# Two six-block groups of each down projection as seven products of halves, between plain groups of 4, 3 and 3 blocks

## The chip, the cores and the metric

The kernel runs on one core of a Trainium2 chip. The metric is the device time of one launch in microseconds. Its engines are named as the profile names them: PE is TensorE (matmuls; PEld is its weight load), DVE is VectorE, ACT is ScalarE, POOL is GpSimd, SP is SyncE, which here issues the DMAs.

## The reference, cut to what matters

One decoder layer over 1024 tokens of width 1024, all in float32. Two of its stages are gated feed-forward blocks with 2816 = 22 x 128 hidden columns; the change lies in them. Between them stands the mixer (attention and a linear recurrence, merged), behind the second the last stage (a gated embedding and the last norm).

```python
def swiglu(x, w_in, w_out):
    gate, up = jnp.split(x @ w_in, 2, axis=-1)
    return (jax.nn.silu(gate) * up) @ w_out
...
        h = h + 0.5 * swiglu(rms_norm(h, norm_ffn1[layer]), w_ffn1_in[layer], w_ffn1_out[layer])
...
        h = h + 0.5 * swiglu(rms_norm(h, norm_ffn2[layer]), w_ffn2_in[layer], w_ffn2_out[layer])
...
```

## The kernel before, in words

Activations are kept transposed: a block is a tile of 128 features (partitions) by 1024 tokens, in two halves of 512 tokens (`HALVES`). Each operand is split into a high and a low part of a narrower type: a product of one 128x128 weight block with 512 tokens is three matmuls (high with high, high with low, low with high). ACT casts the high part (`whi`, `xh`, `gh`), DVE subtracts it to get the low part (`wlo`, `xl`, `gl`).

A half step is one call of `swiglu(n, ...)`, n = 1 for FFN1 and 2 for FFN2. It has two stages.

*Gates.* The 22 hidden blocks are worked off one after the other, as gate units. Units 0 and 1 are plain (`product8`). Units 2 to 21 go by `product7`, a Strassen-like scheme: gate and up columns are the two halves on the one side, the two token halves on the other, and seven products of half the depth (four blocks, three passes, so 12 matmuls each, 84 in a unit) replace eight. Its operands are sums: `wsum` of weights (DVE, then split into parts) and `xsum` of inputs (made once, in class `Halves`). Products are numbered 1 to 7; `a`, `b`, `e`, `g`, `f` are PSUM banks, product 4 adds into product 1's bank after ACT has copied that out as `p`; `u` tiles are partial results that DVE adds. A table `before` hangs extra work on a step of the unit. What to do with the four results is told by an object: `Gated` multiplies by the norm (`rstd`), applies silu and the gate product on POOL (`u*rstd`, `a*u`), and spills the block to DRAM (`aspill`). In FFN1 the norm is not known yet when units 0 and 1 are done, so `keep` copies their sums out of PSUM on ACT, and `rest` evaluates them later, in unit 3 at steps 4 and 6. In FFN2 `all` evaluates units 0 and 1 at once.

*Down.* The 22 blocks are summed in groups (`GROUPS`, 6, 6, 5 and 5 blocks before). For each group and each of the eight output columns c, `gemm` runs blocks x 3 passes x 2 halves matmuls into two PSUM banks, and DVE then adds half of them to the residual tile `hT[c]` (one SCALAR_TENSOR_TENSOR a half). Blocks come back from DRAM as `araw` (`fetch`) and are split into `gh`, `gl` (`part`), one block a column while the previous group runs. In the final group each eviction is followed by the next stage's input (`xgh` on ACT, `xgl` on DVE) and the squares for its norm (`sq` on ACT, added to `acc` on POOL, the very last half on DVE). The next stage's first weights are split in the last two columns: on DVE for the mixer, on POOL for the last stage (`ple`).

`stats_later(acc, a, b)` puts two steps on a side list that PE's k loop counts off: transposes of `acc` with ident, a reduction and a reciprocal square root on DVE (`st_v`, `st_r`), transposes of `st_r`, and the broadcast `rstd`. Before, FFN2's end calls it twice.

DVE and ACT instructions run in the order in which the code is written (class `InOrder`; their line in the profile is therefore always L44). The instructions of PE, POOL and SP are ordered by a scheduler. Pools bound what runs ahead: 38 block tiles of 128x1024, three raw weight tiles (`wraw`), seven split weight tiles, five scratch tiles, eight PSUM banks. `ensure` prepares weights one or two steps ahead in the order of a plan.

In the profile PE's plain matmuls carry line L260 (`gemm_steps`), those of `product7` L280, those of the last stage L1212.

## Time and profile before

| | |
|---|---|
| median of three runs (2228.82 to 2231.6) | 2228.9 us |
| profiled execution, its own time | 2230.69 us |
| its span | 2228.9 us |
| PE busy | 2192.9 us (98%) |
| DVE busy | 1352.5 us (61%) |
| ACT busy | 716.2 us (32%) |
| POOL busy | 442.9 us (20%) |
| FFN1's down stage in the trace | 455.5 to 694.8 us |
| FFN2's down stage in the trace | 1846.05 to about 2085.3 us |

The chain of waits follows the work that ended last back to the beginning; a row of PE there says that nothing but PE itself held it up in that time. The timeline gives each instruction's start and length, and in brackets how long the engine had idled before and for whom. The granted clock is a share of TensorE's full speed of 2.4 GHz.

### The profile page before, as it was taken

The page shows a single profiled execution, that of the slowest core. Times are in us where ns is not written, and L with a number is a line of the kernel's source. Part 1 is how long each engine was busy: PE and PEld are TensorE (multiplying, and loading weights), DVE is VectorE, ACT ScalarE, POOL GpSimd, SP SyncE. Part 2 cuts the span into 40 slices and gives each one's busy share as a digit, 9 for nine tenths or more (in the row PEclk, how much of TensorE's full clock was granted, in tenths as well). Part 3 has the DMA queues.
Part 4 walks back from the last instruction along what each step waited for, and adds up shares of the span by engine and source line. Part 5 has one row for each costly group of instructions (what it writes and reads, how often), then busy time and mean ns, then how long its engine had stood idle before and what let it go on. Part 6 is the DMA issues. An engine that isn't in the chain of part 4 may idle for free.

```text
span 2228.9 us, 26842 instructions
## 1 busy us (share of the span) xinstructions
PE 2192.9 (98%) x10644; PEld 1821.4 (82%) x10644; DVE 1352.5 (61%) x1947; ACT 716.2 (32%) x1191; POOL 442.9 (20%) x233
## 2 busy tenths in 40 slices
PE   8899999999999999999999999999999999999997
PEld 7687888888888888888888888878888888888887
DVE  6777777753345665466674354677777775334545
ACT  6423222231123443322222233332222223122444
POOL 0222222200012000122220122212222220001443
PEclk9999999999999999999999999999999999999999
DMA  9223222272223121111124434212222227221322
GB/s 279 85 86 112 89 85 78 89 266 93 76 79 123 39 67 57 35 32 36 32 67 133 148 108 142 84 58 86 85 85 85 85 96 256 95 70 51 95 75 87
DMA packets 258448, 213.37 MB, mean 96 GB/s; under 512 B 16049, under 2 KB 231442, under 8 KB 258322
## 3 DMA queue, kind: packets, MB, share of 16 engines
q1 hardware_dynamic: 258322, 211.65, 29.7%
q8 instruction: 84, 1.38, 0.3%
q14 instruction: 42, 0.34, 0.1%
HBM read 163.37 MB, written 49.82 MB: 96 GB/s over the span
## 4 chain that ended last, share of the span: by engine, by line
PE 85%; DVE 9%; ACT 2%; issue 1%; POOL 1%; DMA 1%; SPq 0%; ACTq 0%; DVEq 0%; POOLq 0%
PE ps L260 43%; PE ps L280 32%; PE ps L1212 3%; DVE at L44 2%; DVE wlo L44 1%; PE ps L392 1%; PE ps L897 1%; DVE rk L44 1%; PE ps L845 1%; DVE hT L44 1%; DVE xsum L44 1%; PE ps L1251 1%; DVE wsum L44 1%; ACT whi L44 1%; PE ps L884 1%
## 5 line engine op out<-in xcount | busy, mean ns | idle before, releaser
L280 PE MATMUL ps<-xh,whi 128*128 128x512 f32 x800 | 312.8, 391 | 4.0 <-ACT p L44 4.0
L280 PE MATMUL ps<-xh,wlo 128*128 128x512 f32 x800 | 311.8, 390 | 0.6 <-DVE wlo L44 0.5
L280 PE MATMUL ps<-xl,whi 128*128 128x512 f32 x800 | 312.0, 390 | 0.0
L44 ACT CAST whi<-wraw 128x1024 fp32r<-128x1024 f32 (+3 forms) x190 | 174.7, 924 | 346.8 <-PE ps L260 293.5
L658 POOL TENSOR_TENSOR u<-u,rstd 128x1024 f32<-128x1024 f32 x44 | 121.3, 2757 | 653.2 <-ACT a L44 428.6
L44 DVE SCALAR_TENSOR_TENSOR hT<-ps,hT 128x512 f32<-128x512 f32 x128 | 82.5, 686 | 243.0 <-PE ps L260 243.0
L260 PE MATMUL ps<-gh,wlo 128*128 128x512 f32 x704 | 217.1, 389 | 0.0
L260 PE MATMUL ps<-gl,whi 128*128 128x512 f32 x704 | 217.0, 389 | 0.0
L260 PE MATMUL ps<-gh,whi 128*128 128x512 f32 x704 | 216.8, 389 | 0.0
L44 DVE TENSOR_TENSOR wlo<-wraw,whi 128x1024 fp32r<-128x1024 f32 (+3 forms) x174 | 188.6, 1088 | 46.4 <-ACT whi L44 43.4
L260 PE MATMUL ps<-xgh,whi 128*128 128x512 f32 x608 | 197.1, 403 | 0.0
L44 DVE TENSOR_TENSOR wlo<-wsum,whi 128x1024 fp32r<-128x1024 f32 x80 | 134.2, 1678 | 94.5 <-ACT whi L44 94.5
L260 PE MATMUL ps<-xgh,wlo 128*128 128x512 f32 x608 | 190.6, 392 | 0.0
L260 PE MATMUL ps<-xgl,whi 128*128 128x512 f32 x608 | 190.2, 392 | 0.0
L280 PEld LDWEIGHTS ps<-xh,whi 128*128 128x128 f32 x800 | 150.5, 188 | 37.7 <-ACT p L44 6.1
L280 PEld LDWEIGHTS ps<-xh,wlo 128*128 128x128 f32 x800 | 150.6, 188 | 32.8 <-DVE wlo L44 1.5
L280 PEld LDWEIGHTS ps<-xl,whi 128*128 128x128 f32 x800 | 150.6, 188 | 30.9
L44 ACT CAST whi<-wsum 128x1024 fp32r<-128x1024 f32 x80 | 84.2, 1052 | 271.1 <-DVE wsum L44 271.1
L260 PEld LDWEIGHTS ps<-gh,wlo 128*128 128x128 f32 x704 | 132.0, 188 | 27.7 <-DVE wlo L44 0.4
L260 PEld LDWEIGHTS ps<-gl,whi 128*128 128x128 f32 x704 | 132.1, 188 | 27.5
L260 PEld LDWEIGHTS ps<-gh,whi 128*128 128x128 f32 x704 | 132.0, 188 | 27.6
L260 PEld LDWEIGHTS ps<-xgl,whi 128*128 128x128 f32 x608 | 113.6, 188 | 23.9
(253 smaller groups left out, 3832.5 us busy)
## 6 DMA issues: line engine op xcount, KB each, us to landing
wraw<-in_w_ffn_in_dram SPq DMA_DIRECT2D x88, 512.0 KB, 3.9
aspill<-a SPq DMA_DIRECT2D x44, 512.0 KB, 2.9
araw<-aspill SPq DMA_DIRECT2D x44, 512.0 KB, 4.9
wraw<-in_w_in_dram SPq DMA_DIRECT2D x34, 512.0 KB, 3.9
hspill<-hT SPq DMA_DIRECT2D x24, 512.0 KB, 6.3
wraw<-in_w_ffn_out_dram SPq DMA_DIRECT2D x32, 384.0 KB, 4.2
hT<-hspill SPq DMA_DIRECT2D x24, 512.0 KB, 10.2
wraw<-in_w_ffn_out_dram SPq DMA_DIRECT2D x32, 320.0 KB, 3.2
```

The lines of the kernel that those rows point to most:

```text
L44: return self.tc.keep_in_program_order(method(*args, **kwargs))
L260: nc.tensor.matmul(ps[b], wk, xk[:, HALVES[b]], start=(k == 0 and n == 0), stop=(k == kc - 1 and n == 2))
L280: nc.tensor.matmul(ps, a[:, ks], b, start=first and k + n == 0, stop=k == 3 and n == 2, skip_group_check=not first)
L392: nc.tensor.matmul(ps[b], w, xs[b][part], start=i == 0 and m == 0, stop=i == DC - 1 and m == 2)
L658: nc.gpsimd.tensor_mul(self.u, self.u, R["rstd"])
L845: nc.tensor.matmul(ps[:, off:(m + 1) * 256], q[j][0][:, n * P:(n + 1) * P], ak[j][part][:, k0:k1], start=part == 0, stop=part == 1)
L884: nc.tensor.transpose(pt[:, a * P:(a + 1) * P], s[:, (4 * j + a) * P:(4 * j + a + 1) * P], ident)
L897: nc.tensor.matmul(po[64 * j:64 * j + 64, m * P:(m + 1) * P], av[:, (n - 1 + kb) * P + 64 * j:(n - 1 + kb) * P + 64 * j + 64], st[:, (2 * ...
L1212: nc.tensor.matmul(ps, wk, xk[:, sl], start=(k == 0 and n == 0), stop=(k == kc - 1 and n == 2))
L1251: nc.tensor.matmul(self.pp, wps[k][j][:, c * P:(c + 1) * P], pt[k][m][:, self.sl], start=(k + i == 0), stop=(k + i == 3))
```

## The change

The groups become (4, plain), (6, halves), (3, plain), (6, halves), (3, plain). A halves group runs `product7` on pairs of output columns c and c + 4, with the six blocks as two threes: seven products of three blocks and three passes, 63 matmuls, for two columns. Its weights are prepared by `halves_step`, now for any size (768 columns of raw weights, sums of 384). A new class `Down` adds the four results to `hT` with seven SCALAR_TENSOR_TENSOR a unit.

The inputs of a halves group are three pairs of blocks. While the plain group ahead of it runs, `pairs_steps` loads them (`get`), splits their quarters (`put`), forms their four sums of 512 columns each (`sums`), and splits these (`rest`). The sums are made on DVE for the first halves group and on POOL for the second. While a halves group runs, the three blocks of the next plain group are fetched and split, at steps of its second to fourth unit.

The last gate unit fetches and splits blocks earlier, and `hT` tiles are loaded three ahead in place of all at once. In FFN1 the copies of unit 1's sums (`us[1].keep`) move behind product 3 of unit 2, and `us[1].rest` moves from unit 3, step 6, to unit 4, step 4. In FFN2 `us[1].all` moves to the same step of unit 2. At FFN2's end the statistics are made once.

```diff
-    GROUPS = (6, 6, 5, 5)
+    GROUPS = ((4, False), (6, True), (3, False), (6, True), (3, False))
...
+        for gn, halves in GROUPS:
+            for c in PAIRED if halves else range(DC):
+                yield f"{'half' if halves else 'down'}{n}.{f0}.{c}", gn, load_cols(w_down, c * P, P, f0, gn)
...
+            eng = eng or nc.vector
...
-            6: [lambda: squares((4, 5)), lambda: load_rows((6, 7))], 7: [lambda: ensure(where["gate1.2"], 2)]}))
+            6: [lambda: squares((4, 5)), lambda: load_rows((6, 7))], 7: [lambda: ensure(where["gate1.2"], 2)]})
         return {
-            2: {1: [xt[3].p13], 3: [lambda: squares((6, 7)), first_r], 5: [first_rstd]},
-            3: {4: [us[0].rest], 6: [us[1].rest]}}
+            2: {1: [xt[3].p13], 3: [lambda: squares((6, 7)), first_r, lambda: us[1].keep(*ps)], 5: [first_rstd]},
+            3: {4: [us[0].rest]}, 4: {4: [us[1].rest]}}
...
+        def pairs_steps(f0, gn, pairs):
+            half = gn // 2
+
+            def get(j):
+                for k in range(2):
+                    f = f0 + half * k + j
+                    fetch(f)
+                    pairs[j].x[k] = araw.pop(f)
+
+            def put(j):
+                pairs[j].put_seven()
+                pairs[j].sums(nc.gpsimd if f0 > GROUPS[0][0] else nc.vector)
+
+            def rest(j):
+                pairs[j].p24()
+                pairs[j].p13()
+
+            order = ((get, 0), (get, 1), (put, 0), (put, 1, get, 2), (rest, 0), (put, 2), (rest, 1), (rest, 2))
+            return [[lambda f=f, j=j: f(j) for f, j in zip(o[::2], o[1::2])] for o in order]
...
+            def add(self, k, b, *terms):
+                h = hT[self.c + 4 * k][:, HALVES[b]]
+                for t in terms:
+                    nc.vector.scalar_tensor_tensor(h, t, 0.5, h, ALU.mult, ALU.add)
+
+            def c11(self, a):
+                self.add(0, 0, a)
+
+            def c22(self, g, u4):
+                self.add(1, 1, g, u4)
+
+            def c12(self, f, u4):
+                self.add(0, 1, f, u4)
+
+            def c21(self, g, u2):
+                self.add(1, 0, g, u2)
...
+            if halves:
+                todo = [f1 + i for i in range(GROUPS[gi + 1][0])]
+                for c in range(4):
+                    before = {}
+                    if c == 1:
+                        before = {5: [lambda: fetch(todo[0])]}
+                    elif c == 2:
+                        before = {2: [lambda: part(todo[0]), lambda: fetch(todo[1])], 6: [lambda: part(todo[1]), lambda: fetch(todo[2])]}
+                    elif c == 3:
+                        before = {3: [lambda: part(todo[2])]}
+                    product7(f"half{n}.{f0}.{c}", pairs[f0], Down(c), before)
+                del pairs[f0]
+                continue
...
+                pairs[f1] = [Halves() for _ in range(GROUPS[gi + 1][0] // 2)]
+                steps = pairs_steps(f1, GROUPS[gi + 1][0], pairs[f1])
...
-        us[1].all(*ps)
-        return {}
+        return {2: {3: [lambda: us[1].all(*ps)]}}
 
     hT, xg, acc = swiglu(2, xt, R_PLE, lambda c, h: None, second_units)
-    stats_later(acc, 9, 6)
-    stats_later(acc, 9, 6)
+    stats_later(acc, 8, 8)
```

Three places show how the instructions move. The first is ACT's queue in FFN1's unit 2. `a` and `u` are unit 1's sums, `whi<-wsum` the two casts of weight sums of unit 2, `p` the copy that product 4 waits for. Before:

```order
L44 CAST whi<-wsum 128x1024
L44 COPY a<-ps 128x512 x2
L44 COPY u<-ps 128x512 x2
L44 CAST xh<-xsum 128x1024
L44 CAST whi<-wsum 128x1024
L44 COPY p_667<-ps 128x512
L44 ACTIVATE xrow,xv<-xrow 128x1024 x2
L44 CAST whl<-wraw 128x512
L44 CAST whi<-wraw 128x1024
L44 COPY rstd<-ps 128x512 x2
```

After:

```order
L44 CAST whi<-wsum 128x1024
L44 CAST xh<-xsum 128x1024
L44 CAST whi<-wsum 128x1024
L44 COPY p_663<-ps 128x512
L44 ACTIVATE xrow,xv<-xrow 128x1024 x2
L44 COPY a<-ps 128x512 x2
L44 COPY u<-ps 128x512 x2
L44 CAST whl<-wraw 128x512
L44 CAST whi<-wraw 128x1024
L44 COPY rstd<-ps 128x512 x2
```

The four copies stand behind `p` and the row statistics now, where they stood ahead of `xh` and the second cast.

The second place is the entry to the second down group of six in FFN1, on DVE. Before, in the third group, weights, evictions and block splits take turns:

```order
L44 TENSOR_TENSOR wlo<-wraw,whi 128x768
L44 SCALAR_TENSOR_TENSOR hT<-ps,hT 128x512 x2
L44 TENSOR_TENSOR wlo<-wraw,whi 128x640
L44 SCALAR_TENSOR_TENSOR hT<-ps,hT 128x512 x2
L44 TENSOR_TENSOR wlo<-wraw,whi 128x640
L44 SCALAR_TENSOR_TENSOR hT<-ps,hT 128x512 x2
```

After, from the plain group of three (the last two columns' evictions) into the first unit of the second halves group:

```order
L44 TENSOR_TENSOR wlo<-wraw,whi 128x768
L44 SCALAR_TENSOR_TENSOR hT<-ps,hT 128x512 x2
L44 TENSOR_TENSOR xl<-xsum,xh 128x1024 x2
L44 TENSOR_TENSOR wsum<-wraw 128x384
L44 TENSOR_TENSOR wsum<-wsum,wraw 128x384
L44 TENSOR_TENSOR wlo<-wsum,whi 128x768
L44 SCALAR_TENSOR_TENSOR hT<-ps,hT 128x512 x2
L44 TENSOR_TENSOR wsum<-wraw 128x384
L44 TENSOR_TENSOR wsum<-wraw,wsum 128x384
L44 TENSOR_TENSOR wlo<-wsum,whi 128x768
L44 TENSOR_TENSOR u_4540<-ps,p_4528 128x512
L44 TENSOR_TENSOR whl<-wraw,whl 128x384
```

Splits of the pair sums, weight sums and two weight splits stand between the last evictions. The sums themselves, `xsum`, are on POOL; its queue between FFN1's last gate unit and the final group's squares was, before:

```order
L658 TENSOR_TENSOR u<-u,rstd 128x1024
L659 TENSOR_TENSOR a<-a,u 128x1024
L658 TENSOR_TENSOR u<-u,rstd 128x1024
L659 TENSOR_TENSOR a<-a,u 128x1024
L474 TENSOR_TENSOR acc_4584<-acc_4584,sq 128x512 x13
L989 TENSOR_TENSOR rq_6862<-rq_6862,rf_6742 128x1024
```

and is now, with the second and third pair's eight sums like the four shown left out ahead of the squares:

```order
L670 TENSOR_TENSOR u<-u,rstd 128x1024
L671 TENSOR_TENSOR a<-a,u 128x1024
L670 TENSOR_TENSOR u<-u,rstd 128x1024
L671 TENSOR_TENSOR a<-a,u 128x1024
L364 TENSOR_TENSOR xsum<-araw 128x512
L365 TENSOR_TENSOR xsum<-araw 128x512
L366 TENSOR_TENSOR xsum<-xsum,araw 128x512
L367 TENSOR_TENSOR xsum<-araw,xsum 128x512
```

The four sums of a pair follow the last gate product directly.

The third place is DVE at the end of FFN1's final group, where the mixer's first weights (1024 columns) are split. Before:

```order
L44 TENSOR_TENSOR wlo<-wraw,whi 128x640
L44 SCALAR_TENSOR_TENSOR hT<-ps,hT 128x512 x2
L44 SCALAR_TENSOR_TENSOR xgl<-hT,pcol,xgh 128x512 x2
L44 TENSOR_TENSOR wlo<-wraw,whi 128x1024
L44 SCALAR_TENSOR_TENSOR hT<-ps,hT 128x512 x2
L44 SCALAR_TENSOR_TENSOR xgl<-hT,pcol,xgh 128x512 x2
L44 TENSOR_TENSOR wlo<-wraw,whi 128x1024
```

After:

```order
L44 TENSOR_TENSOR wlo<-wraw,whi 128x384
L44 SCALAR_TENSOR_TENSOR hT<-ps,hT 128x512 x2
L44 SCALAR_TENSOR_TENSOR xgl<-hT,pcol,xgh 128x512 x2
L44 TENSOR_TENSOR wlo<-wraw,whi 128x1024
L44 SCALAR_TENSOR_TENSOR hT<-ps,hT 128x512 x2
L44 SCALAR_TENSOR_TENSOR xgl<-hT,pcol,xgh 128x512 x2
L44 TENSOR_TENSOR wlo<-wraw,whi 128x1024
```

The order is the same; the weights ahead have 384 columns in place of 640, and PE has three blocks in place of five to cover a row of evictions.

## Rows read from the trace of the kernel before

**Rows 1.** The page: busy time of the engines; a DMA issue (count, KB, landing us).
```profile
PE 2192.9 (98%) x10644; PEld 1821.4 (82%) x10644; DVE 1352.5 (61%) x1947; ACT 716.2 (32%) x1191; POOL 442.9 (20%) x233
...
wraw<-in_w_ffn_out_dram SPq DMA_DIRECT2D x32, 384.0 KB, 4.2
```

**Rows 2.** Chain of waits in order of time: start us, us, what ran.
```profile
215.87 239.65 PE ps L280 x1056
455.53 246.25 PE ps L260 x1086
...
1846.05 235.37 PE ps L260 x1038
```

**Rows 3.** Stretches: window and length, busy us of each engine, granted clock, DMA share, GB/s.
```profile
74.00:78.00 4.00, 2.64 (x16) 2.03 (x15) 3.06 (x15) 2.43 (x5) 0.00 (x0) 1.00 0.01 3
106.00:110.00 4.00, 4.00 (x11) 3.15 (x12) 3.18 (x2) 0.92 (x2) 2.37 (x1) 0.57 0.12 48
1472.00:1476.00 4.00, 4.00 (x13) 3.11 (x12) 4.00 (x5) 0.92 (x1) 0.04 (x1) 0.62 0.70 241
```

**Rows 4.** Timeline of PE: start us, us, instruction, then idle time and its releaser.
```profile
72.54 0.50 PE L280 MATMUL ps<-xh,whi 128*128 128x512 f32 x1 [0.81 <-ACT p L44]
...
76.91 1.09 PE L451 MATMUL ps<-ident,st_r 128*128 128x128 f32 x8 [1.36 <-DVE st_r L44]
...
105.88 0.47 PE L280 MATMUL ps<-xh,whl 128*128 128x512 f32 x1 [2.65 <-DVE u L44]
...
1471.51 0.73 PE L280 MATMUL ps<-xh,whi 128*128 128x512 f32 x1 [2.14 <-ACT p L44]
...
2093.21 1.03 PE L413 MATMUL ps<-ident,acc 128*128 128x128 f32 x8
...
2099.12 1.06 PE L451 MATMUL ps<-ident,st_r 128*128 128x128 f32 x8 [0.77 <-DVE st_r L44]
```

**Rows 5.** Timeline of ACT and DVE in FFN1's first seven-product units.
```profile
65.47 1.06 ACT L44 COPY a<-ps 128x512 f32<-128x512 f32 x2
...
100.81 2.59 DVE L44 TENSOR_TENSOR wlo<-wraw,whi 128x1024 fp32r<-128x1024 f32 x1 [1.46 <-ACT whi L44]
```

**Rows 6.** Groups of instructions by shape: count, busy us, mean ns, idle us before.
```profile
L44 DVE SCALAR_TENSOR_TENSOR hT<-ps,hT 128x512 f32<-128x512 f32 x128 | 82.5, 686 | 243.0 <-PE ps L260 243.0
...
L44 DVE TENSOR_TENSOR wsum<-wraw 128x512 f32<-128x512 f32 x80 | 55.1, 689 | 0.0
...
L44 DVE TENSOR_TENSOR wlo<-wraw,whi 128x768 fp32r<-128x768 f32 x32 | 30.5, 952 | 0.0
...
L44 ACT CAST gh<-araw 128x512 fp32r<-128x512 f32 x88 | 49.5, 617 | 31.9 <-DMA araw<-aspill 31.5
...
L955 POOL TENSOR_TENSOR rq<-rq,decays 128x512 f32<-128x512 f32 x24 | 30.3, 1262 | 39.3 <-issue 28.5 <-ACT q L44 6.6 <-POOL rq L955 3.5
```

**Rows 7.** Timeline of DVE and POOL in FFN2's unit 2.
```profile
1466.94 2.90 DVE L44 TENSOR_TENSOR wsum<-wraw,wsum 128x512 f32<-128x512 f32 x1
...
1466.57 2.71 POOL L658 TENSOR_TENSOR u<-u,rstd 128x1024 f32<-128x1024 f32 x1 [19.75 <-DVE u L44]
```

**Rows 8.** Timeline of POOL in FFN2's last plain group.
```profile
2081.22 2.57 POOL L474 TENSOR_TENSOR acc<-acc,sq 128x512 f32<-128x512 f32 x2 [1.88 <-ACT sq L44]
2083.74 2.40 POOL L93 TENSOR_TENSOR wlo<-wraw,whi 128x1024 fp32r<-128x1024 f32 x1
```

**Rows 9.** Timeline of DVE, then PE, at FFN1's last two columns and the mixer's start.
```profile
681.18 1.29 DVE L44 SCALAR_TENSOR_TENSOR hT<-ps,hT 128x512 f32<-128x512 f32 x2 [2.07 <-PE ps L260]
...
685.26 2.30 DVE L44 TENSOR_TENSOR wlo<-wraw,whi 128x1024 fp32r<-128x1024 f32 x1 [1.18 <-ACT whi L44]
...
694.78 1.29 DVE L44 SCALAR_TENSOR_TENSOR hT<-ps,hT 128x512 f32<-128x512 f32 x2 [0.42 <-PE ps L260]
...
697.99 1.39 DVE L44 TENSOR_TENSOR acc<-acc,sq 128x512 f32<-128x512 f32 x1 [0.31 <-ACT sq L44]
...
701.62 1.03 PE L413 MATMUL ps<-ident,acc 128*128 128x128 f32 x8
```

102 lines of the change are left out of this document (56 added, 46 removed).

## The prediction, made before the kernel had run

> **What bounds the kernel now.** I read the page's table of engines first: TensorE (PE) is busy for 98% of the span [rows 1]. Then the chain of waits in order of time, where one sees that each of the two down stages is one unbroken piece of PE work: 1086 matmuls in 246.25 us and 1038 in 235.37 us, so 0.2268 us for one of 512 columns, with no wait between them [rows 2]. The gate units, which already use seven products, run in one piece too: 1056 matmuls in 239.65 us, or 84 matmuls in 19.05 us a unit [rows 2]. Last I read the stretches by granted clock and PE's own timeline where it does wait, because every wait that the change can touch lies outside the down stages [rows 3, 4]. Counted from these, a matmul taken out of a down stage is 0.2268 us off the end, as long as VectorE (DVE), ScalarE (ACT) and GpSimd (POOL) keep up with the new pace.
>
> **1. Matmuls removed.** A pair of columns over six blocks is 2 x 6 x 3 x 2 = 72 matmuls in the plain way and 7 x 3 x 3 = 63 in seven products. There are four pairs in a group, two such groups in a half step and two half steps: 16 units x 9 = 144 matmuls, 144 x 0.2268 = **-32.7 us**. A unit is 63 x 0.2268 = 14.29 us of PE, a product 2.04, a column over four blocks 5.44 and over three 4.08.
>
> **2. Start of FFN1.** Unit 2 waits 0.81 us for ACT and 1.36 us for the statistics on DVE [rows 4]. Ahead of both stand four ACT copies of unit 1's sums, a pair in 1.06 us and another alike, about 1.9 us in all with their overlap [rows 5]. The change sends them behind product 3; I take 1.4 of the two waits as gone, and not all, since the copies come back later in the same unit. In unit 3 the two `rest` blocks no longer follow each other: the second moves to unit 4. The 2.65 us wait behind a weight split that itself took 2.59 us, and the lower clock after it, end [rows 4, 5]: in the 4 us after that wait PE ran 11 matmuls at a granted 0.57 (the step to 1.2 GHz within the stretch), where 4 / 0.2268 = 17.6 would fit, so 6.6 x 0.2268 = 1.5 us, and 1.6 with the end of it [rows 3]. Of these 4.25 us I keep some 1.45 in each of units 3 and 4, whose POOL multiplies now block DVE once each. Together -1.4 - 4.25 + 2.9 = -2.75, and -1 for the shorter ACT queue ahead of unit 3's first wait: **-3.7 us**. Bounds: all of 0.81 + 1.36 + 4.25 = -6.4, and +1.6 if a new wait lowers the clock again.
>
> **3. Start of FFN2.** Unit 2 waits 2.14 us for a copy on ACT [rows 4]; in the next 4 us PE ran 13 matmuls at a granted 0.62 [rows 3], 4.6 x 0.2268 = 1.0, and 1.4 with what follows that stretch. The copy waits for sums on DVE, which were held by POOL's multiply of unit 1: 2.90 us for an addition against 0.69 [rows 6, 7]. With unit 1's evaluation moved behind product 3, the addition comes ahead of that multiply. **-3.5 us**; bounds -4.5 and, if the moved DVE work (four operations, 2.6 us) meets another wait, 0.
>
> **4. FFN2 to the last stage.** The second copy of the statistics goes: eight transposes of the sum of squares, 1.03 us in their row, eight of st_r alike, and a wait of 0.77 us ahead of those may go [rows 4]: at most 2 x 1.03 + 0.77 = -2.8, with their overlap with the next matmuls -2.4. Against that, the final group has three blocks: POOL needs 2.57 for squares and 2.40 for a weight split, 4.97 us a column, while PE now needs 4.08 [rows 8], so over the last two columns POOL is 1.8 us later against PE; the sum of squares is ready later by about that, and the small loads of the last stage wait on SP behind a weight load that wants a buffer of that split. I set +1.4 for both: **-1.0 us**, bounds -2.8 and, should all 1.8 and a lowered clock's 1.6 come on top, +1.0.
>
> **5. Seven-product groups.** Here nothing of before shows the work itself, so I cost it by rows of like shape. DVE has in a unit nine operations on PSUM or accumulation (two u sums, seven hT), 9 x 0.645 = 5.8; four sums of 384 columns, between 0.5 and 0.69, say 0.55 [rows 6]; three weight splits of 768 at 0.95 and one of 384 at 0.55 [rows 6]: 5.8 + 2.2 + 2.85 + 0.55 = 11.4 of 14.29 us. It fits, as gate units with 19.05 us do; the tight place is the ACT copy `p`, which product 4 (into the same bank) waits for and which stands behind a cast of sums from DVE. By order and durations it ends some 0.45 us before it is wanted in a plain unit. In the third unit of each group two casts of the next blocks stand ahead of it, 0.62 each [rows 6] and 1.1 with their overlap, so 0.65 us of wait; the second group's entry lacks 0.4 us because its `xl` and sums come after the last plain column. One POOL sum that holds a split costs 0.8 more, in the second group. (2 x 0.65 + 0.4 + 0.8) x 2 = **+5.0 us**. Lower bound 0 (the gate units' chain has no wait), upper 16 units x 0.81, the ACT wait of FFN1's unit 2 [rows 4], = +13.
>
> **6. FFN1 to the mixer.** The final group goes from five blocks to three, PE from 6.80 to 4.08 us a column, but its evictions stay. A cycle on DVE and ACT (two hT, two xgl, then the next weights) took 4.08 us from the first hT to the split, which then needed 2.30 beside POOL's squares, 6.38 in all, with weights of 1024 columns [rows 9]. That cycle stays in the last two columns, 2.30 over PE's pace each. With 384 columns the cast, half a microsecond shorter, brings the split forward, and that takes 0.55 to 0.95: 4.1 to 4.5, on average 0.2 over. So DVE falls behind by 6 x 0.2 + 2 x 2.30 = 5.8, and I take 6.1 with the start of the group. Before, the last eviction began with the mixer's first matmul and the sum of squares was ready 697.99 + 1.39 - 694.78 = 4.6 us later, while its transposes were due 6.8 us after [rows 9]. Now it is ready at 6.1 + 4.6 = 10.7: a wait of 3.9 plus 0.1, and after a wait of that length the clock falls as in rows 3, 1.6: **+5.6 us**. Bounds 0, should the weight splits stand elsewhere, and +7.
>
> The second group's twelve 512-column sums of each half step go to POOL at 1.26 us, against 0.69 on DVE [rows 6]: 15.1 us of POOL, which is 80% idle [rows 1]; I cost them at the 0.8 in step 5 alone. The Trainium skill, GPSIMD Engine Reference, section 4.1, says that element-wise work belongs on VectorE, GpSimd being about twice slower with two inputs. The rows agree on the price, 1.26 to 0.69. By that rule the sums would stand on DVE, and the plain three-block group would hold 28 + 8.3 of 32.7 us, some 3.7 us over per half step; by the rows the slower engine is free, so what counts is what it holds up.
>
> **The sum.** -32.7 - 3.7 - 3.5 - 1.0 + 5.0 + 5.6 = -30.3 us. The profiled execution took 2230.7 us, 1.8 more than the median of the runs and 1.8 more than its own span; 2230.7 - 30.3 = 2200.4, in terms of the median 2228.9 - 30.3 = **2198.6 us**.
>
> **Rivals.** A, covers hold: steps 5 and 6 cost nothing beyond 1 us. For it: no wait in any down stage or steady gate unit [rows 2]. Against: step 6's sum is from plain durations. -40.9 + 1 = -39.9: 2189. B, DVE becomes the bound of the plain three-block group: eight columns of weights and hT, 8 x (0.55 + 1.29), and three pairs of splits, 3 x (0.69 + 1.29 + 2.44), are 28 of 32.7 us; if each of POOL's twelve sums holds a DVE operation for all of its 1.26 us, 28 + 15.1 = 43, or 10.4 too much per half step. For it: the addition that starts 0.37 us after a POOL multiply takes 2.90 instead of 0.69 [rows 6, 7]; against: by the order a part of the sums begins already in the last seven-product unit. 2198.6 + 20.8 - 1.6 (step 5's share) = 2218; half of it is 2208. The Trainium skill, SBUF — State Buffer, section Who interferes with whom, has this as a rule: a DVE operation with two SBUF inputs and a GpSimd operation that reads SBUF exclude each other, whichever started first. Rows 7 show just that. C, slower: the chain DVE sum, ACT cast, ACT copy `p`, product 4 sets the pace of every unit. Waits of the size of FFN2's 2.14 us with its 1.4 of lower clock would be 16 x 3.5 = 57 in place of step 5's 5: 2198.6 + 52 = 2250. It decides from (32.7 + 8.2 - 5.6) / 16 = 2.2 us lost a unit; a wait of 1.36 left the clock at 1.00 and one of 2.14 did not [rows 3, 4]. Against: 2.9 us of DVE's 14.29 are free. D, the change doesn't do what it says: the six-block weights or araw blocks land late, since more is read just ahead of use; a load of 384 KB took 4.2 us [rows 1] and two are due in 14.29, so I give it little.
>
> **Chances.** Forecast (2193 to 2206) 0.50, A 0.20, B 0.22 (2207 to 2224), C 0.05, D and others on the slow side 0.03. The range leaves out half of A's better end, B's upper third and C: 2186 to 2216. About 0.2%, 4.5 us, is what a measurement of this kernel tells from no change, so same is 2224.4 to 2233.4: faster 0.91, same 0.04, slower 0.05.
>
> **What would show it.** Step 1: 960 + 1008 matmuls in place of 2112 and both down stages shorter by some 14 us each. Step 2 and 3: no idle time above 1 us in FFN1's units 2 to 4 and FFN2's unit 2, no granted clock below 1 there. Step 5: PE idle time in the seven-product groups of 5 us in all, released by ACT `p` and DVE `wlo`. Step 6: one wait of about 4 us ahead of the sum-of-squares transposes, released by DVE or POOL acc, with a lower clock behind it. B would show as DVE splits above 2 us beside POOL's `xsum`, C as a wait in front of product 4 of every unit. I am wrong if the down stages are not free of waits, or if the starts lose what they gain.

## The result, and the profile after

The changed kernel takes 2204.09 us in the median of four runs (2202.99 to 2204.9), beside 2229.33 us for the kernel before on the same chip: a ratio of 0.9885 (95% interval 0.9871 to 0.9900), 25 us faster. The forecast was 2198.6 us with a range of 2186 to 2216. The profiled execution took 2202.99 us, its span 2201.1, 27.8 us less than the span of before; the stretches below are counted in these two spans.

The page of the changed kernel: busy time of the engines and the chain of waits by engine. In its trace L284 is the line of the seven products and L263 that of the plain matmuls.

```profile
PE 2160.5 (98%) x10484; PEld 1790.5 (81%) x10484; DVE 1530.8 (70%) x2193; ACT 761.2 (35%) x1265; POOL 480.8 (22%) x257
...
PE 75%; DVE 13%; ACT 4%; issue 3%; POOL 2%; DMA 2%; SPq 0%; ACTq 0%; DVEq 0%; POOLq 0%
```

VectorE went from 61% to 70% of the span, PE stayed at 98%, and PE's share of the chain fell from 85% to 75%: the chain now runs more over VectorE and ScalarE. Of [rows 2] only the gate part came back as it was. The chain of waits in order of time (start us, us, what ran) shows the down stage of FFN1 as pieces:

```profile
213.19 239.66 PE ps L284 x1056
...
498.94 32.30 PE ps L284 x141
532.30 22.54 PE ps L284 x98
...
591.62 31.76 PE ps L284 x138
624.43 22.53 PE ps L284 x98
```

141 and 98 matmuls in the first halves group, 138 and 98 in the second, in place of 1086 in one piece. Between them the chain runs over other engines. PE's timeline has these waits where the change is (FFN1's units 3 and 4, the entry of the two halves groups, the mixer's statistics; then the same for FFN2, without the units):

```profile
103.56 0.47 PE L284 MATMUL ps<-xh,whl 128*128 128x512 f32 x1 [1.52 <-ACT a L44]
...
124.15 0.47 PE L284 MATMUL ps<-xh,whl 128*128 128x512 f32 x1 [1.27 <-ACT a L44]
...
498.94 0.50 PE L284 MATMUL ps<-xh,whi 128*128 128x512 f32 x1 [0.53 <-ACT whi L44]
...
590.62 0.50 PE L284 MATMUL ps<-xh,whi 128*128 128x512 f32 x1 [1.11 <-ACT whi L44]
...
689.11 1.21 PE L425 MATMUL ps<-ident,acc 128*128 128x128 f32 x8 [2.71 <-POOL acc L486]
...
1878.11 0.50 PE L284 MATMUL ps<-xh,whi 128*128 128x512 f32 x1 [0.64 <-ACT whi L44]
...
1969.66 0.50 PE L284 MATMUL ps<-xh,whi 128*128 128x512 f32 x1 [0.99 <-ACT whi L44]
...
2066.84 1.20 PE L425 MATMUL ps<-ident,acc 128*128 128x128 f32 x8 [2.10 <-POOL acc L486]
```

The waits of 0.81, 2.65 and 2.14 us of [rows 4] are gone, and the 1.36 us for unit 2's row statistics became 0.78. At FFN2's end the 0.77 us ahead of the transposes of `st_r` gave way to 2.10 us ahead of those of the sum of squares. New are the entry waits of the halves groups, behind ACT's cast of weight sums, and the 2.71 us ahead of the mixer's statistics. The down stage of FFN1 by stretches (halves, plain 3, halves, plain 3), and the 4 us behind the mixer's wait; columns are window, length, busy us of PE, PEld, DVE, ACT and POOL, granted clock, DMA share, GB/s:

```profile
496.20:554.67 58.47, 57.82 (x253) 47.02 (x252) 48.57 (x75) 17.24 (x28) 4.40 (x4) 1.00 0.31 102
554.67:587.31 32.64, 32.64 (x145) 27.03 (x144) 30.22 (x39) 14.01 (x21) 14.71 (x9) 1.00 0.35 109
587.31:646.80 59.49, 58.23 (x254) 46.98 (x252) 48.74 (x77) 17.24 (x28) 0.00 (x0) 1.00 0.24 73
646.80:679.45 32.65, 32.65 (x146) 27.04 (x145) 24.96 (x36) 17.14 (x29) 14.20 (x10) 1.00 0.52 170
689.11:693.11 4.00, 4.00 (x16) 3.22 (x17) 3.46 (x14) 0.00 (x0) 0.00 (x0) 0.70 0.40 121
```

The halves groups hold 58.5 and 59.5 us where 4 x 14.29 = 57.2 are matmuls; VectorE is busy for 30.2 of 32.6 us in the three-block group between them. In the last row PE ran 16 instructions, eight of them short transposes, at a granted 0.70; a variant with the same wait and the full clock (last section) ran 21.

The two spans against each other, by the starts of units and stages on PE (FFN2's units 3 to 21 took 361.8 us in both and are left out):

| stretch | before, us | after, us | change | step and its forecast |
|---|---|---|---|---|
| to FFN1's unit 5 | 129.64 | 126.96 | -2.7 | 2: -3.7 |
| units 5 to 21 | 325.73 | 325.73 | 0.0 | |
| FFN1 down | 239.44 | 226.75 | -12.7 | 1 and 5: -16.3 + 2.5 |
| mixer, to FFN2's unit 2 | 764.90 | 769.71 | +4.8 | 6: +5.6 |
| FFN2's unit 2 | 24.42 | 20.84 | -3.6 | 3: -3.5 |
| FFN2 down | 239.43 | 226.51 | -12.9 | 1 and 5: -16.3 + 2.5 |
| last stage | 143.58 | 142.84 | -0.7 | 4: -1.0 |

These make -27.8 us, against a forecast of -30.3.

### The profile page after: what moved, and what is told of

It is laid out like the page before. It is cut to its first block, busy times and chain, and to the rows that moved or that the text cites. A ratio compares the mean times of both kernels' runs of the same rounds, so it can differ in the third digit from the quotient of the medians.

```text
span 2201.1 us, 27007 instructions
## 1 busy us (share of the span) xinstructions
PE 2160.5 (98%) x10484; PEld 1790.5 (81%) x10484; DVE 1530.8 (70%) x2193; ACT 761.2 (35%) x1265; POOL 480.8 (22%) x257
## 4 chain that ended last, share of the span: by engine, by line
PE 75%; DVE 13%; ACT 4%; issue 3%; POOL 2%; DMA 2%; SPq 0%; ACTq 0%; DVEq 0%; POOLq 0%
PE ps L284 40%; PE ps L263 25%; PE ps L1284 3%; DVE wlo L44 2%; DVE xl L44 2%; DVE hT L44 2%; DVE at L44 2%; ACT whi L44 1%; PE ps L404 1%; DVE wsum L44 1%; PE ps L971 1%; DVE rk L44 1%; DMA araw<-aspill 1%; DVE xsum L44 1%; ACT sq L44 1%
## 5 line engine op out<-in xcount | busy, mean ns | idle before, releaser
L284 PE MATMUL ps<-xh,whi 128*128 128x512 f32 x1040 | 405.9, 391 | 4.7 <-ACT whi L44 3.3
L284 PE MATMUL ps<-xl,whi 128*128 128x512 f32 x1040 | 404.7, 389 | 0.0
L284 PE MATMUL ps<-xh,wlo 128*128 128x512 f32 x1040 | 403.8, 390 | 0.7 <-DVE wlo L44 0.5
L44 ACT CAST whi<-wsum 128x1024 fp32r<-128x1024 f32 (+1 forms) x112 | 110.9, 990 | 420.1 <-DVE wsum L44 420.1
L44 DVE TENSOR_TENSOR wlo<-wsum,whi 128x1024 fp32r<-128x1024 f32 (+1 forms) x112 | 164.0, 1464 | 125.4 <-ACT whi L44 125.4
L284 PEld LDWEIGHTS ps<-xh,whi 128*128 128x128 f32 x1040 | 195.2, 188 | 49.8 <-ACT whi L44 5.5
L284 PEld LDWEIGHTS ps<-xh,wlo 128*128 128x128 f32 x1040 | 195.2, 188 | 43.5 <-DVE wlo L44 2.8
L284 PEld LDWEIGHTS ps<-xl,whi 128*128 128x128 f32 x1040 | 195.2, 188 | 39.9
L263 PE MATMUL ps<-xgh,whi 128*128 128x512 f32 x608 | 197.5, 404 | 0.0
L263 PE MATMUL ps<-xgl,whi 128*128 128x512 f32 x608 | 191.1, 393 | 0.0
L263 PE MATMUL ps<-xgh,wlo 128*128 128x512 f32 x608 | 191.0, 393 | 0.0
L284 PE MATMUL ps<-xh,whl 128*128 128x512 f32 x416 | 137.5, 390 | 3.0 <-ACT a L44 3.0
L44 DVE TENSOR_TENSOR u<-ps,u 128x512 f32<-128x512 f32 x136 | 93.0, 684 | 65.6 <-PE ps L284 65.0
L263 PEld LDWEIGHTS ps<-xgh,wlo 128*128 128x128 f32 x608 | 114.0, 189 | 24.1
L263 PEld LDWEIGHTS ps<-xgl,whi 128*128 128x128 f32 x608 | 114.0, 188 | 24.1
L284 PE MATMUL ps<-xhl,whi 128*128 128x512 f32 x416 | 128.3, 390 | 0.4 <-ACT whi L44 0.4
L263 PEld LDWEIGHTS ps<-xgh,whi 128*128 128x128 f32 x608 | 108.2, 189 | 21.0 <-issue 2.7
L44 DVE SCALAR_TENSOR_TENSOR hT<-ps,hT 128x512 f32<-128x512 f32 x160 | 105.0, 682 | 25.9 <-PE ps L263 17.6
```

The costliest lines, as they stand in the source:

```text
L44: return self.tc.keep_in_program_order(method(*args, **kwargs))
L263: nc.tensor.matmul(ps[b], wk, xk[:, HALVES[b]], start=(k == 0 and n == 0), stop=(k == kc - 1 and n == 2))
L284: nc.tensor.matmul(ps, a[:, ks], b, start=first and k + n == 0, stop=k == last and n == 2, skip_group_check=not first)
```

## Experiments

The variants are named, in the order below, e1_starts; e2_vsum, e5_gsum and e11_third (the sums); e3_p13late, e9_early3 and e10_order2 (the entry); e4_mixlate and e6_final4 (the statistics); e8_rest6, e12_best (three moves together) and e14_best (the last kernel). All runs stand beside the kernel before on the same chip; the changed kernel's own ratio is 0.9885. The interval of a ratio is about 0.0015 to either side, some 3 us, so differences of 2 us between variants are read from the stretches of their traces, not from times.

### The starts alone

The kernel before, with the two moved evaluations of gate unit 1 and nothing else.

```diff
-        us[1].keep(*product8(1, 1, xt, PAIRED, {
+        ps = product8(1, 1, xt, PAIRED, {
...
-            2: {1: [xt[3].p13], 3: [lambda: squares((6, 7)), first_r], 5: [first_rstd]},
-            3: {4: [us[0].rest], 6: [us[1].rest]}}
+            2: {1: [xt[3].p13], 3: [lambda: squares((6, 7)), first_r, lambda: us[1].keep(*ps)], 5: [first_rstd]},
+            3: {4: [us[0].rest]}, 4: {4: [us[1].rest]}}
...
-        us[1].all(*ps)
-        return {}
+        return {2: {3: [lambda: us[1].all(*ps)]}}
```

> The kernel before with the two moved evaluations of gate unit 1 alone (FFN1's keep and rest, FFN2's all); groups 6, 6, 5, 5 and the rest as before. Theory (the starts are a term of their own): FFN1's units 2 to 4 and FFN2's unit 2 gain what the two traces show there, 2.7 and 3.6 us, with PE's 2.65 and 2.14 us waits and the lower clock behind them gone: 2229.3 - 6.3 = 2223.0. Rival (the gain at the starts comes with the groups, since their first loads and hT loads in the last gate unit were moved too): within 1 us of 2229.3.

Measured: 2224.0 us, ratio 0.9972 (0.9963 to 0.9982), -6.3 us. FFN1's units 2 to 4 took 64.5 us in place of 67.7 (-3.2), FFN2's unit 2 20.8 in place of 24.4 (-3.6). The starts are a term of their own, a quarter of the whole gain, and have nothing to do with the halves groups.

### What the sums cost, and on which engine

The twelve sums of the second group on VectorE, so that GpSimd does none:

```diff
-                pairs[j].sums(nc.gpsimd if f0 > GROUPS[0][0] else nc.vector)
+                pairs[j].sums(nc.vector)
```

> The changed kernel with the second group's sums on VectorE too. Theory (VectorE is full in the three-block group from the arrival of the third pair on, and POOL's sums cost it only what they hold up, some 2.3 us there): twelve sums of 0.69 us are 8.3 us more VectorE work per half step, less 2.3 held up, less about 3 us in which it now idles: PE waits some 3 us more at each second halves group's entry, with a lower clock behind it perhaps, so 2204.1 + 6 to + 10 = 2210 to 2214. Rival (exclusion between the two engines costs as much as the work itself): no change, 2203 to 2206.

Measured: 2215.41 us, ratio 0.9933 (0.9919 to 0.9948), 11 us slower than the changed kernel. PE's timeline at the second groups' entry in FFN1 and FFN2 and in the three-block group ahead, and the 4 us behind the first entry wait (columns as above):

```profile
594.32 0.80 PE L284 MATMUL ps<-xh,whi 128*128 128x512 f32 x1 [3.55 <-ACT whi L44]
...
1980.21 0.80 PE L284 MATMUL ps<-xh,whi 128*128 128x512 f32 x1 [3.55 <-ACT whi L44]
...
584.54 0.74 PE L263 MATMUL ps<-gh,wlo 128*128 128x512 f32 x2 [0.96 <-DVE wlo L44]
...
594.32:598.32 4.00, 4.00 (x9) 2.93 (x10) 3.06 (x5) 0.55 (x1) 0.00 (x0) 0.50 0.00 0
```

The entry wait is 3.55 us in place of 1.11 and 0.99, and the first unit of the group 7.2 us over its 14.29 in place of 1.9 and 1.6. Of these 5.3 and 5.6 us about half is the longer wait and half the clock behind it, which stands at 0.50: 9 matmuls in 4 us, where 17.6 would fit. A further 0.96 us of waiting stands in each three-block group, which takes 33.9 us in place of 32.6. So sums of 8.3 us a half step became 13 us of time in the two down stages together, and a part of that is the clock. The Trainium skill's rule that element-wise work belongs on VectorE (GPSIMD Engine Reference, section 4.1) would have chosen this kernel; here the measurement decides against it, because VectorE is the full engine in that stretch and GpSimd is not.

All sums of both groups on GpSimd:

```diff
-                pairs[j].sums(nc.gpsimd if f0 > GROUPS[0][0] else nc.vector)
+                pairs[j].sums(nc.gpsimd)
```

> The changed kernel with the first group's sums on GpSimd as well. Theory (entry waits are VectorE's queue in the plain group ahead): the first groups' plain group loses twelve sums of 0.6 to 0.7 us from VectorE, 7.9 us, and pays some 2.3 for splits held up; the first units' excess of 0.9 and 1.0 us goes: 2204.1 - 1.9 = 2202.2. Rival (POOL's third pair and its hold on the splits set the entry, as in the second groups): their excess grows to the 1.6 to 1.9 of the second groups, 2205.7.

Measured: 2207.25 us, ratio 0.9898 (0.9883 to 0.9913). The first units of the first groups went from 0.9 and 1.0 us over to 1.9 and 1.9; the second groups', whose code is the same, were 1.6 and 1.6 over. That is the rival: taking 7.9 us of sums from VectorE did not shorten the entry, it made it the same as the second groups'. Another 1.8 us of this trace lie in the last stage, where the clock fell behind the wait of 2.10 us (last section).

The second group's third pair alone on VectorE:

```diff
-                pairs[j].sums(nc.gpsimd if f0 > GROUPS[0][0] else nc.vector)
+                pairs[j].sums(nc.gpsimd if f0 > GROUPS[0][0] and j < 2 else nc.vector)
```

> The changed kernel with the second group's third pair summed on VectorE, the first two pairs on POOL. Theory (in the full part of VectorE's queue POOL's four sums hold up splits for 2.3 us, nearly the 2.6 us that the sums themselves would take there): the second groups' excess is the same within 0.7 us, 2203 to 2206. Rival (POOL's sums are as good as free, as all twelve on VectorE cost 11 us): 2.6 us more a group, with a lower clock perhaps, 2209 to 2211.

Measured: 2205.58 us, ratio 0.9885 (0.9870 to 0.9900), the second groups' first units 2.2 and 2.0 us over in place of 1.9 and 1.6. So four sums on VectorE, 2.6 us of it, cost about as much as four on GpSimd: the 0.3 us between them is no more than FFN1's entry differs between traces of kernels with the same code there (1.6 to 2.4 us over without a lower clock; FFN2's 1.6 to 1.7). The reason stands in the changed kernel's trace, VectorE then GpSimd in the three-block group, first during the eight sums of the first two pairs and behind them, then during the four of the third:

```profile
558.15 1.65 DVE L44 TENSOR_TENSOR wlo<-wraw,whi 128x384 fp32r<-128x384 f32 x1
...
562.80 1.29 DVE L44 SCALAR_TENSOR_TENSOR hT<-ps,hT 128x512 f32<-128x512 f32 x2 [1.35 <-PE ps L263]
...
572.17 3.58 DVE L44 TENSOR_TENSOR xl<-xsum,xh 128x1024 fp32r<-128x1024 f32 x2
575.67 1.65 DVE L44 TENSOR_TENSOR wlo<-wraw,whi 128x384 fp32r<-128x384 f32 x1
...
572.69 1.97 POOL L365 TENSOR_TENSOR xsum<-araw 128x512 f32<-128x512 f32 x1 [0.26 <-DMA araw<-aspill]
574.74 2.16 POOL L366 TENSOR_TENSOR xsum<-xsum,araw 128x512 f32<-128x512 f32 x1
```

The two `xl` splits take 3.58 us in place of 2.35, and the weight split 1.65 in place of 0.55: 2.3 us of VectorE go in waiting for the sums beside them. The first eight sums hold VectorE up too: three weight splits take 1.16, 1.65 and 1.65 us in place of 0.55 each. But behind them VectorE still idles, 1.35 us for PE and twice 0.52, so PE loses nothing; the third pair's inputs come when VectorE has no idle time left until the group's entry.

That the hold sets the entry is shown by kernels with the same code there, because it is not the same length in every trace. In the kernel with three moves together (below, e12_best), VectorE in FFN1's three-block group and PE at the second group's entry:

```profile
570.63 4.25 DVE L44 TENSOR_TENSOR xl<-xsum,xh 128x1024 fp32r<-128x1024 f32 x2
...
589.77 0.50 PE L285 MATMUL ps<-xh,whi 128*128 128x512 f32 x1 [1.80 <-ACT whi L44]
```

The two `xl` splits take 0.67 us longer than in the changed kernel, and PE waits 0.69 longer, 1.80 us in place of 1.11. In e8_rest6 they take 4.07 us, and PE waits 1.61.

### The entry of a halves group

One move: the split of the third pair's T1 and T3, wanted from product 3 on, issued behind the group's first weight sums.

```diff
             def rest(j):
                 pairs[j].p24()
-                pairs[j].p13()
+                if j < 2:
+                    pairs[j].p13()
...
                 ensure(where[f"half{n}.{f1}.0"], 2)
+                pairs[f1][2].p13()
```

> The changed kernel with one move: the split of the third pair's T1 and T3 (needed from product 3 on) is issued behind the halves group's first weight sums and not ahead of them. Theory (the entry waits of 0.5 to 1.1 us before product 2, and the ones behind them, are the VectorE queue: two xl splits of 1.22 us stand ahead of the weight sums): one split of 1.2 us off that queue; entry excess of the first unit falls from 0.9, 1.9, 1.0, 1.6 us to 0.3 or less in the first groups and 0.7 in the second: 5.4 to 2.0 in all, 2204.1 - 3.4 = 2200.7. Rival (the wait is for the late third pair, whose inputs land 17 us before the group, on POOL): entry excess of the second groups unchanged, 2203.5.

Measured: 2202.62 us, ratio 0.9877 (0.9861 to 0.9894). The expectation was wrong: the first units were 0.8, 1.7, 1.1 and 1.7 us over, 5.3 in all in place of 5.4. The wait before product 2 went and came back before products 3 and 4. VectorE's queue is late as a whole, and the order of its last pieces decides only which product notices. The second groups' excess stayed, as the rival had it. (Behind the mixer's statistics its trace gained 1.8 us and in the last stage it lost 1.6, both a matter of the clock; that belongs to the last section.)

Both groups' third pair one column earlier:

```diff
-            order = ((get, 0), (get, 1), (put, 0), (put, 1, get, 2), (rest, 0), (put, 2), (rest, 1), (rest, 2))
+            order = ((get, 0), (get, 1), (put, 0, get, 2), (put, 1), (put, 2, rest, 0), (rest, 1), (rest, 2), ())
```

> The changed kernel with the third pair loaded one column earlier and split one column earlier, so that nothing new is left for the last column of the plain group. Theory (entry waits are the last 15 us of VectorE's queue, while it idled 2.9 us before the third pair was there): the second groups' excess falls from 1.9 and 1.6 us to 0 to 0.5, the first groups' from 0.9 and 1.0 to 0: 2204.1 - 4.5 = 2199.6. Rival (the wait is a fixed chain of sum, cast, split and product at the group's entry, which an earlier third pair doesn't shorten, as moving one split only moved the wait by a product): 2203 to 2205, excess as before.

Measured: 2205.02 us, ratio 0.9889 (0.9875 to 0.9904), nothing gained. VectorE in the three-block group, and PE's waits in the first plain group and at the second group's entry:

```profile
568.80 1.73 DVE L44 TENSOR_TENSOR xhl<-araw,xhl 128x512 fp32r<-128x512 f32 x1
570.46 3.49 DVE L44 TENSOR_TENSOR xl<-araw,xh 128x512 fp32r<-128x512 f32 x2
...
487.74 0.72 PE L263 MATMUL ps<-gh,wlo 128*128 128x512 f32 x2 [0.89 <-DVE wlo L44]
...
591.94 0.50 PE L284 MATMUL ps<-xh,whi 128*128 128x512 f32 x1 [1.56 <-ACT whi L44]
```

The first groups' entry did become free of waits, but 0.89 us (and 1.11 in FFN2) stood in the plain group instead, behind a weight split that came late. In the second group `put` of the second pair now met the third pair's sums: splits of 1.97 us in all took 5.1, and the entry got no earlier.

The second group's preparation alone one column earlier throughout:

```diff
+            if f0 > GROUPS[0][0]:
+                order = ((get, 0, get, 1), (put, 0), (put, 1, get, 2), (rest, 0), (put, 2), (rest, 1), (rest, 2), ())
```

> The changed kernel with the second group's preparation alone one column earlier throughout (the first group's as it was). Theory (VectorE's queue in the three-block group is the bound, but it idles 2.9 us before the third pair is there): that idle time is used, the second groups' excess falls from 1.9 and 1.6 us to 0.5 or less, and no new wait stands in the plain group: 2204.1 - 2.5 = 2201.6. Rival (work that comes earlier meets more of POOL's sums, as with both groups one column earlier, where two splits took 3.49 us in place of 1.29): excess as it was or above, 2204 to 2206.

Measured: 2200.56 us, ratio 0.9863 (0.9849 to 0.9878). The second groups' first units are 1.1 and 0.9 us over in place of 1.9 and 1.6, half of what was expected. The collision of the two engines went the other way round here, VectorE then GpSimd:

```profile
583.14 2.36 DVE L44 TENSOR_TENSOR xl<-xsum,xh 128x1024 fp32r<-128x1024 f32 x2 [2.44 <-ACT xh L44]
...
576.80 3.86 POOL L366 TENSOR_TENSOR xsum<-xsum,araw 128x512 f32<-128x512 f32 x1
```

The third pair's sums hold no work of VectorE up, but three of them take 3.4 to 3.9 us on GpSimd, and VectorE then idles 2.44 us for them (through ACT's cast `xh`); in FFN2 it is the same. The second groups gain 1.5 us by this. The first groups' first units, whose code is the same, are 1.1 and 1.6 us over in this trace in place of 0.9 and 1.0, so the two down stages together gain only 0.7; 1.6 us more lie in the mixer, where the clock did not fall.

### The statistics behind the final group

The mixer's statistics are counted off later, and `flush`, which evicts the previous product, is left out once, ahead of the mixer's weights `ak`.

```diff
-        flush()
+        if key != "ak":
+            flush()
         return prepared[i].pop("w")
...
-    stats_later(acc)
+    stats_later(acc, 8, 4)
```

> The changed kernel with the mixer's statistics later: transposes of the sum of squares behind the mixer's first product (8 blocks) in place of 5 blocks, st_r 4 blocks later, and the first product's eviction one product later. Theory (step 6: PE waits 2.71 us for the sum of squares, which lags because the final group's evictions are slower than its three blocks, and runs at a lower clock behind it): the sum is ready 9.7 us after the mixer's start, the transposes are due at 10.9: wait and lower clock gone, 2204.1 - 4.3 = 2199.8. Rival (the wait only moves, to the transposes of st_r or to PSUM banks held by the later eviction): 2203 to 2205 with an idle time of 2 us at one of those.

Measured: 2198.62 us, ratio 0.9859 (0.9844 to 0.9873). PE's timeline at both sets of transposes:

```profile
689.38 1.03 PE L426 MATMUL ps<-ident,acc 128*128 128x128 f32 x8
...
695.71 1.03 PE L464 MATMUL ps<-ident,st_r 128*128 128x128 f32 x8
```

Neither has an idle time ahead of it, and the mixer takes 764.96 us from its first matmul to FFN2's unit 2, as it did before the change (764.90), in place of 769.71. The whole of step 6, 4.8 us, is this one wait and the clock behind it. With the wait and without the fall of the clock (e10_order2 above) the mixer takes 768.1 us, so 3.2 are the wait and 1.6 the clock.

The other way to remove it is to give PE more to do a column. Groups of 3, 6, 3, 6 and 4, both groups' sums on GpSimd as above, and the fetches and splits of blocks adjusted to the sizes (left out here):

```diff
-    GROUPS = ((4, False), (6, True), (3, False), (6, True), (3, False))
+    GROUPS = ((3, False), (6, True), (3, False), (6, True), (4, False))
...
-                pairs[j].sums(nc.gpsimd if f0 > GROUPS[0][0] else nc.vector)
+                pairs[j].sums(nc.gpsimd)
...
```

> Groups of 3, 6, 3, 6 and 4 in place of 4, 6, 3, 6 and 3, with both groups' sums on GpSimd. Theory (the waits for the sums of squares come from final evictions of 4.37 us a column against 4.08 of PE): with four blocks PE takes 5.44, only the last two columns lag, 2 x 0.9, so the sum is ready 1.8 + 4.6 = 6.4 us after the mixer's start where 6.8 are allowed: FFN1's wait of 2.71 us and the lower clock behind it go, FFN2's 2.10 falls below 1; the first groups' entry becomes like the second's, 1.8 in place of 0.95 each: 2204.1 - 4.3 - 1.3 + 1.7 = 2200.2. Rival (the sum is late for POOL's and VectorE's hold on each other in the last two columns alone): both waits stay above 2 us, 2205.8.

Measured: 2215.95 us, ratio 0.9935 (0.9918 to 0.9951), 11 us slower than the changed kernel, where 4 faster were expected. PE's timeline at the mixer's statistics, then in the first plain group and at the first halves group:

```profile
695.69 1.03 PE L425 MATMUL ps<-ident,acc 128*128 128x128 f32 x8
...
475.41 0.74 PE L263 MATMUL ps<-gh,wlo 128*128 128x512 f32 x2 [1.47 <-DVE wlo L44]
...
494.76 0.50 PE L284 MATMUL ps<-xh,whi 128*128 128x512 f32 x1 [3.57 <-ACT whi L44]
```

The expected part came: both statistics stand without a wait, and the mixer takes 764.99 us. The other part was mis-sized. A first plain group of three blocks leaves VectorE so little that PE waits inside it (1.47 and 1.69 us in FFN1, 2.35 and 1.27 in FFN2) and for 3.57 us at the entry; the first units are 6.1 and 5.9 us over. A part of the loss is the clock, which fell behind both entry waits (0.66 and 0.57) and behind the 2.35 us (0.57). The second three-block group does not suffer that. Its sums begin earlier, in the halves group ahead of it; that this is the reason was not tested.

### One late evaluation, and three moves together

The late evaluations of gate units 0 and 1 in FFN1, each at step 6 of its unit in place of step 4.

```diff
-            3: {4: [us[0].rest]}, 4: {4: [us[1].rest]}}
+            3: {6: [us[0].rest]}, 4: {6: [us[1].rest]}}
```

> The changed kernel with both late evaluations of FFN1's plain gate units at step 6 of units 3 and 4 in place of step 4. Theory (the waits of 1.52 and 1.27 us before product 7 come from one POOL multiply of 2.40 us that holds one weight split, 2.58 in place of 1.22): at step 6 that multiply stands beside additions with a PSUM operand; both waits go, 2204.1 - 2.8 = 2201.3. Rival (it then holds up the next weight sums, and the wait comes back before product 2 or 3 of the following unit): 2203 to 2205.

Measured: 2201.92 us, ratio 0.9876 (0.9861 to 0.9891). In the changed kernel VectorE's weight split of unit 3 stands beside the late evaluation's multiply on GpSimd:

```profile
99.62 2.58 DVE L44 TENSOR_TENSOR wlo<-wraw,whi 128x1024 fp32r<-128x1024 f32 x1 [1.47 <-ACT whi L44]
...
98.73 2.40 POOL L671 TENSOR_TENSOR a<-a,u 128x1024 f32<-128x1024 f32 x1 [4.59 <-ACT a L44]
```

The split takes 2.58 us in place of 1.22. With the move the waits of 1.52 and 1.27 us are gone, and smaller ones stand before product 4 of units 4 and 5, the first of them:

```profile
112.37 0.50 PE L284 MATMUL ps<-xh,whi 128*128 128x512 f32 x1 [0.51 <-ACT p L44]
```

Units 3 to 5 are 2.3 us over in place of 4.0, a gain of 1.7; a part of the wait moved on, as the rival had it.

Three moves together: the mixer's statistics (`stats_later(acc, 8, 4)`, with the `flush` held back), the late evaluations at step 6, both as above, and FFN2's statistics:

```diff
-    stats_later(acc, 8, 8)
+    stats_later(acc, 10, 6)
```

> The changed kernel with the mixer's statistics later (8 blocks, then 4), both late evaluations of FFN1 at step 6, and FFN2's transposes of the sum of squares 2 blocks later (10 and 6). Theory (three separate waits of PE): 2204.1 - 5.5 - 2.2 - 1.4 = 2195.0; FFN2's wait of 2.10 falls to 0.8. Rival (one of them only covered another, or a later st_r takes over in the last stage): 2197 to 2199.

Measured: 2204.03 us, ratio 0.9875 (0.9858 to 0.9891): no better than the changed kernel. VectorE, then PE, in its last stage:

```profile
2068.06 2.48 DVE L44 TENSOR_TENSOR pl<-ps,ph 128x512 fp32r<-128x512 f32 x4
2070.45 1.28 DVE L44 TENSOR_REDUCE st_v<-ps 128x4 f32<-128x512 f32 x2
...
2074.92 1.06 PE L464 MATMUL ps<-ident,st_r 128*128 128x128 f32 x8 [3.84 <-DVE st_r L44]
```

With ten blocks the statistics are issued behind the embedding's splits (`pl`, four in 2.48 us, and as many `wpl`) in VectorE's program order and no longer ahead of them; st_r is late, and PE waits 3.84 us for it, at a granted 0.63 behind it, where it had waited 2.10 for the sum; the last stage takes 147.7 us in place of 142.8. The other two moves held in their places (units 3 to 5 are 2.3 us over, the mixer takes 764.96 us). But the last stage is not the whole loss: FFN1's second group waits the 1.80 us shown above, the clock falls there to 0.67, and its first unit is 4.0 us over in place of 1.9. None of the three moves touches that entry. In e8_rest6, too, the wait there is 1.61 us, in the other kernels with the same code there 1.0 to 1.1; what makes the difference is open.

So the last kernel leaves FFN2's statistics as they were and takes the three moves that held by themselves: the mixer's statistics, the late evaluations, the second group's order.

> The changed kernel with the three moves that held by themselves: the mixer's statistics later (8 blocks, then 4), both late evaluations of FFN1 at step 6, the second group's preparation one column earlier; FFN2's statistics stay at 8 and 8. Theory (three separate waits): from the stretches of the single runs, the mixer 2.7 and its lower clock 1.6, gate units 1.7, second groups 1.5, so 2204.1 - 7.5 = 2196.6. Rival (the last kernel with three moves showed that one of them may only uncover another wait): 2199 or above, with a new wait above 1 us outside the places known.

Measured: 2196.31 us (2194.3 to 2197.5), ratio 0.9843 (0.9829 to 0.9857), 8 to 9 us faster than the changed kernel and 34 faster than the kernel before. Units 3 to 5 are 2.3 us over, the second groups' first units 1.1 each, the mixer takes 765.1 us. The profiled execution gained 5.7 us on the changed kernel's, less than the medians say; the clock fell behind FFN2's wait in the one and not in the other, and its last stage takes 144.4 us in place of 142.8. It is the fastest version found.

## Why the prediction was right

The time lies in the range, 5.5 us above the forecast, and the mechanism was the forecast one. Of the 5.5 us, 2.5 are in the terms (-27.8 in the spans, where -30.3 was forecast), the largest of them a step 5 that was 2 us too small. The rest lies between executions: the profiled one of before was 1.8 us above the median that the forecast was set against, that of after 1.1 below its own. Some luck is in the single terms: whether the clock falls behind a wait of 2 to 3 us, 1.6 us each time, was not foreseeable from the rows (last section). It fell in the mixer, as step 6 had it, and not in the last stage, as step 4 had it.

**Step 1, matmuls removed.** Right. The second and fourth unit of every halves group run in 14.3 us, and the plain columns at 0.2268 us a matmul; -32.7 us are there, less what step 5 takes.

**Step 2, FFN1's start.** -3.2 us in units 2 to 4, forecast -3.7. The waits of 1.52 and 1.27 us in units 3 and 4 are the 1.45 each that the step kept, from the cause that it named: a GpSimd multiply across one weight split. The other half microsecond is not the change's: unit 2 began 0.5 us later in this execution, and among the variants, whose code up to there is the same, it began anywhere from 61.3 to 62.9 us.

**Step 3, FFN2's start.** -3.6 us, forecast -3.5; the same with the starts alone. Right.

**Step 4, FFN2 to the last stage.** -0.7 us, forecast -1.0. The sum of squares is 2.10 us late; in traces in which the clock fell behind that wait, the last stage took 144.4 to 144.7 us, which would be +0.8 to +1.1. The reason given, GpSimd's squares and weight splits in the last two columns, is right and goes further than stated: they also hold VectorE's `xgl`, and are held by it. VectorE and GpSimd there:

```profile
2055.95 3.96 DVE L44 SCALAR_TENSOR_TENSOR xgl<-hT,pcol,xgh 128x512 fp32r<-128x512 f32 x2 [0.52 <-ACT xgh L44]
...
2056.53 2.84 POOL L93 TENSOR_TENSOR wlo<-wraw,whi 128x1024 fp32r<-128x1024 f32 x1
```

Two `xgl` take 3.96 us in place of the 1.42 that they take in the columns before, and a weight split 2.84 in place of the 2.40 of [rows 8].

**Step 5, seven-product groups.** +7.0 us, forecast +5.0: the term that was mis-sized. Its 0.65 us for the third unit's two casts was 0.42. Its 0.4 us for the second group's entry and 0.8 for one held split were 1.9 and 1.6 together, and the first group's entry, put at none, was 0.9 and 1.0. The step took VectorE's queue as all but caught up at the start of the group; the runs on the entry show that VectorE comes out of the plain group late. In the second group the third pair's sums hold it up by 2.3 us, in three splits and not in one.

**Step 6, FFN1 to the mixer.** +4.8 us, forecast +5.6. The evictions came at the pace that the step had worked out, 4.38 us a column (4.1 to 4.5 forecast) against 4.08, and 6.30 in the last two (6.38 forecast). VectorE's timeline, with GpSimd's squares across the weight split:

```profile
668.07 1.28 DVE L44 SCALAR_TENSOR_TENSOR hT<-ps,hT 128x512 f32<-128x512 f32 x2
...
671.60 0.93 DVE L44 TENSOR_TENSOR wlo<-wraw,whi 128x384 fp32r<-128x384 f32 x1 [0.64 <-ACT whi L44]
672.45 1.28 DVE L44 SCALAR_TENSOR_TENSOR hT<-ps,hT 128x512 f32<-128x512 f32 x2
...
678.75 1.28 DVE L44 SCALAR_TENSOR_TENSOR hT<-ps,hT 128x512 f32<-128x512 f32 x2
...
685.05 1.28 DVE L44 SCALAR_TENSOR_TENSOR hT<-ps,hT 128x512 f32<-128x512 f32 x2
...
670.78 2.90 POOL L486 TENSOR_TENSOR acc<-acc,sq 128x512 f32<-128x512 f32 x2 [1.49 <-ACT sq L44]
```

The transposes could start 9.7 us after the mixer's first matmul, where the sum was forecast for 10.7; so the wait was 2.71 us in place of 3.9, and the lower clock came as forecast.

**The rivals.** A was refuted by the entry and mixer waits. B was weighed rightly as something between: GpSimd's twelve sums hold VectorE up in places, not throughout, and moving all of them to VectorE costs more than it saves. C did not occur: no unit but the first and the third of a group waits at all. Nor did D: none of PE's waits above 0.3 us in the two down stages is for a load.

**The signs.** Two of them fail as they are worded, against the prediction's own terms: units 3 and 4 of FFN1 do have waits above 1 us (step 2 keeps 1.45 in each), and the down stages are not free of waits (step 5 counts 5 us there). And step 5's waits were to be released by ACT's `p` and DVE's `wlo`; `p` is right for the third unit, whose product 4 starts as that copy ends, but the larger part, at the entries, is released by ACT's cast of weight sums (`whi`), which itself waits for VectorE to make them.

## What to carry to other kernels

A saving on the bounding engine holds to the last matmul where the other engines keep pace, and is lost at the seams, where their queue comes out of the previous stage late; walk the full engine's queue through the seam before trusting the sum. Work on a slower, idle engine is cheap only where what it holds up on the full engine can still be made good: eight sums that held VectorE's splits up cost PE nothing, because VectorE came to wait for PE behind them; four more just ahead of the seam held it up by 2.3 us, and 0.7 us more of that was 0.7 us more of waiting on PE. A wait moved to another place in one program order often only uncovers the next one, so move one at a time and look at the trace.
